# The opening of a two-layer diffusion step: a written-out order, squares summed by matmul, filter biases added by matmul

## Chip, core and metric

The kernel runs on one core of a Trainium2 chip. The metric is device time in microseconds (us), the median of three runs. A row of the trace is one execution taken by the hardware profiler. The core has TensorE (PE, whose weight loads are listed apart as PEld), VectorE (DVE), ScalarE (ACT), GpSimd (POOL) and SyncE (SP). SP and ACT here also issue transfers; an issue stands in their queue like any other instruction. Each engine takes its instructions in the order in which the program has them.

## What is computed

One inference step of a backbone with two layers, width 1024, on 512 latent tokens and 128 context tokens (640 columns in all). A layer is

```python
shift, scale, gate = split(silu(cond) @ W_mod + b_mod)      # one set for latents, one for context
h = rms_norm(x) * (1 + scale) + shift
u_a, g_a, u_b, g_b, u_c, g_c, m = split(h @ W_in)
y_a = GLU(S5_bidir(u_a)) * silu(g_a)                        # state-space scan in both directions
y_b = Hyena2(u_b) * silu(g_b)                               # long convolution with learnt filters, by FFT
y_c = MultiPool(u_c) * silu(g_c)
x = x + gate * W_out(sum_b sigmoid(m_b) * (y_b @ W_br_b))

# the filters of a layer (two orders x 512 channels) depend on weights alone:
f = sin(freq * (z @ w1 + b1)); f = sin(freq * (f @ w2 + b2))
filt = (f @ w3) * window                                    # then its Fourier transform
y = irfft(rfft(u) * rfft(filt)) + u * bias                  # bias folded into the filter's centre tap
```

The latent tokens get a position embedding before the first layer. All data are float32. Large products are made of three matmuls on a high and a low part of each operand.

## The kernel before

The 1024 features lie as 8 blocks (`kk`) of 128 partitions, tokens along the free axis in two halves of 320. A scheduler orders each engine's instructions from the program's order, from data dependences and from the number of buffers of each tile. Only the opening of layer 0 matters here, up to the first input product `u_a`, whose result the scan (S5) waits for. The pieces are these.

- `mlp` makes `fh`, the two sine layers under the filters (`fh_91` in the order rows).
- `load_x0` adds the position embedding to `X`. `square` squares each block and half on ACT (tile `sq`) and adds the squares up on DVE, so that one `acc` and one `sq` tile per half are left; `rsum` then makes their column sums by 20 matmuls (tile `ssq`), and `rinv` the reciprocal root and its copy over all partitions (`rdg`, `rbc`, `rr`).
- `mod_chunk` loads a fourth of the modulation weights of a shift or scale in four transfers of 512 KB (tile `wm`, four buffers), makes 8 matmuls (`modp`; a row of the trace counts two for each) and copies them (`mp`). `mod_turn` turns the result into columns (`modt`, then `smod` and `sg` on DVE). Chunks 0 and 1 are the shift, 2 and 3 the scale.
- `filter` makes one of four filters: five matmuls (`fw` x4, `fwp`), the window on DVE (`hx`, `hq`), two additions of a bias row (`br`, 1x256), `fold`, the split into `fhi`, `flo`, `fhp`, `flp` on ACT and DVE, 42 matmuls with the Fourier matrix (`fps`), copies (`hs`) and four stores (`hd`) in SP's queue.
- `s5_disc` and `s5_disc2` make the scan's coefficients (`pw`, `rs`, `bb`, `pi`, `po`, `ph`; stores `pwd`, `rsd`), much of it on ACT as copies. `s5_open` makes the scan's first matrices, with copies `bp` and `bf`.
- `make_h` makes `h` in 24 pieces, three column ranges for each block (`ht` on DVE, `hhi` on ACT, `hlo` on DVE; blocks 3 and 6 start on POOL), and `u_a` multiplies it with the first 512 columns of `W_in` in 192 matmuls (`mm`). Their weights arrive as `wr` and are split to `wh` (ACT) and `wl` (DVE). The result goes out as `ud` and comes back as `ug`, with which the scan's first matmul (`pz`) begins.

## Time and profile before

| | |
|---|---|
| median of 3 runs | 1528.59 us (1523.9 to 1529.53) |
| the profiled execution | 1527.04 us |
| its span, first to last instruction | 1525.3 us |
| mean granted TensorE clock | 0.982 |
| PE, DVE, ACT, POOL busy | 94%, 73%, 44%, 34% |
| first `u_a` matmul, last `u_a` matmul | 78.08 us, 128.14 us |
| first `pz` matmul | 145.3 us |

The span is 1.74 us shorter than the execution's own time. In the windows view a row is a stretch of the span: its length, then the busy time of each engine with the number of instructions, the granted TensorE clock (1.00 is full speed), the share of the DMA engines and GB/s.

### The profile page before, as it was taken

The page shows a single profiled execution, that of the slowest core. Times are in us where ns is not written, and L with a number is a line of the kernel's source. Part 1 is how long each engine was busy: PE and PEld are TensorE (multiplying, and loading weights), DVE is VectorE, ACT ScalarE, POOL GpSimd, SP SyncE. Part 2 cuts the span into 40 slices and gives each one's busy share as a digit, 9 for nine tenths or more (in the row PEclk, how much of TensorE's full clock was granted, in tenths as well). Part 3 has the DMA queues.
Part 4 walks back from the last instruction along what each step waited for, and adds up shares of the span by engine and source line. Part 5 has one row for each costly group of instructions (what it writes and reads, how often), then busy time and mean ns, then how long its engine had stood idle before and what let it go on. Part 6 is the DMA issues. An engine that isn't in the chain of part 4 may idle for free.

```text
span 1525.3 us, 28396 instructions
## 1 busy us (share of the span) xinstructions
PE 1441.0 (94%) x10812; PEld 1366.2 (90%) x10812; DVE 1107.4 (73%) x1962; ACT 672.7 (44%) x1454; POOL 514.9 (34%) x462
## 2 busy tenths in 40 slices
PE   3999999999999999999998998999999999999997
PEld 1688899999999998898897887999999999999996
DVE  7896987955777796544567779887567778866665
ACT  3474545434333344344334744544443334344443
POOL 0033435400343334553221444552004443266401
PEclk9799999999999999999999999999999999999998
DMA  9535222244222348543653442222522223322154
GB/s 317 185 109 145 78 69 75 70 129 122 92 79 70 94 127 273 173 149 125 205 177 109 136 119 77 79 74 91 162 85 80 84 70 111 111 84 83 39 176 153
DMA packets 121904, 182.41 MB, mean 120 GB/s; under 512 B 34104, under 2 KB 58440, under 8 KB 121257
## 3 DMA queue, kind: packets, MB, share of 16 engines
q1 hardware_dynamic: 117177, 174.25, 37.2%
q0 software_dynamic: 1152, 5.77, 1.2%
q8 instruction: 85, 1.39, 0.4%
q10 hardware_dynamic: 3440, 0.59, 0.2%
q14 instruction: 50, 0.41, 0.1%
HBM read 154.75 MB, written 25.80 MB: 118 GB/s over the span
## 4 chain that ended last, share of the span: by engine, by line
PE 67%; DVE 17%; DMA 5%; issue 5%; ACT 3%; POOL 2%; SPq 1%; POOLq 0%; DVEq 0%; ACTq 0%
PE mm L261 14%; PE mm L263 14%; PE mm L262 14%; PE mm L333 3%; PE mm L335 3%; PE mm L334 3%; DVE wl L239 3%; PE modp L404 2%; PE inva L1189 1%; PE invb L1189 1%; PE yp L1020 1%; DVE kk L1006 1%; DVE i L918 1%; DVE vx L1049 1%; DVE kk L1005 1%
## 5 line engine op out<-in xcount | busy, mean ns | idle before, releaser
L261 PE MATMUL mm<-hhi,wh 128*128 128x320 f32 x1408 | 442.0, 315 | 5.6 <-ACT raw L1040 2.7
L263 PE MATMUL mm<-hhi,wl 128*128 128x320 f32 x1408 | 438.7, 313 | 6.6 <-DVE wl L239 4.4
L262 PE MATMUL mm<-hlo,wh 128*128 128x320 f32 x1408 | 439.7, 312 | 1.0 <-DVE hlo L659 0.4
L239 DVE TENSOR_TENSOR wl<-wr,wh 128x512 fp32r<-128x512 f32 x316 | 262.8, 833 | 111.1 <-ACT wh L238 108.0
L238 ACT CAST wh<-wr 128x512 fp32r<-128x512 f32 x316 | 195.5, 619 | 260.7 <-PE mm L262 196.8
L261 PEld LDWEIGHTS mm<-hhi,wh 128*128 128x128 f32 x1408 | 266.9, 190 | 11.4 <-ACT raw L1040 4.3
L263 PEld LDWEIGHTS mm<-hhi,wl 128*128 128x128 f32 x1408 | 266.7, 190 | 8.9 <-DVE wl L239 5.9
L262 PEld LDWEIGHTS mm<-hlo,wh 128*128 128x128 f32 x1408 | 267.0, 190 | 3.2 <-DVE hlo L659 1.6
L261 PE MATMUL mm<-mhi,wh 128*128 128x320 f32 x256 | 79.7, 315 | 3.6 <-DVE X L1312 2.8
L262 PE MATMUL mm<-mlo,wh 128*128 128x320 f32 x256 | 80.1, 314 | 0.5 <-DVE mlo L242 0.4
L263 PE MATMUL mm<-mhi,wl 128*128 128x320 f32 x256 | 79.3, 313 | 0.4 <-DVE wl L239 0.4
L917 POOL TENSOR_TENSOR ow<-cw,po 128x512 f32<-128x512 f32 x32 | 38.9, 1233 | 109.0 <-PE yp L1020 101.3
L919 POOL TENSOR_TENSOR i<-i,i 128x1024 f32<-128x1024 f32 x16 | 43.9, 2747 | 69.3 <-DVE i L917 40.8
L239 DVE TENSOR_TENSOR wl<-ws,wh 128x512 fp32r<-128x512 f32 x48 | 42.2, 880 | 31.5 <-ACT wh L238 30.5
L1290 POOL TENSOR_TENSOR macc<-macc,mth 128x320 f32<-128x320 f32 x32 | 36.3, 1139 | 83.9 <-DVE mth L1288 83.8
L1288 DVE SCALAR_TENSOR_TENSOR mth<-mth,mm 128x320 f32<-128x320 f32 x64 | 31.1, 485 | 43.1 <-PE mm L263 43.1
L333 PE MATMUL mm<-hhi,wh 128*128 128x320 f32 x192 | 59.9, 312 | 0.0
L335 PE MATMUL mm<-hhi,wl 128*128 128x320 f32 x192 | 59.9, 312 | 0.0
L334 PE MATMUL mm<-hlo,wh 128*128 128x320 f32 x192 | 59.8, 311 | 0.0
L238 ACT CAST wh<-ws 128x512 fp32r<-128x512 f32 x48 | 29.8, 620 | 57.3 <-PE mm L262 29.6
L261 PEld LDWEIGHTS mm<-mhi,wh 128*128 128x128 f32 x256 | 48.5, 191 | 5.3 <-DVE X L1312 3.1
L1290 POOL TENSOR_TENSOR acc<-acc,mth 128x320 f32<-128x320 f32 x32 | 38.0, 1189 | 44.3 <-DVE mth L1288 34.3
(422 smaller groups left out, 3752.7 us busy)
## 6 DMA issues: line engine op xcount, KB each, us to landing
wr<-w_in SPq DMA_DIRECT2D x224, 256.0 KB, 2.9
wm<-w_mod SPq DMA_DIRECT2D x48, 512.0 KB, 4.7
wr<-w_out SPq DMA_DIRECT2D x48, 256.0 KB, 3.0
hd<-hs SPq DMA_DIRECT2D x32, 256.0 KB, 2.2
hsr<-hd SPq DMA_DIRECT2D x32, 256.0 KB, 2.8
mt<-kd SPq DMA_DIRECT2D x128, 32.0 KB, 1.8
wr<-w_br_a SPq DMA_DIRECT2D x16, 256.0 KB, 2.5
wr<-w_br_b SPq DMA_DIRECT2D x16, 256.0 KB, 3.2
```

The lines of the kernel that those rows point to most:

```text
L238: nc.scalar.copy(hi, src)
L239: nc.vector.tensor_tensor(out=lo, in0=src, in1=hi.bitcast(F32), op=ALU.subtract)
L261: nc.tensor.matmul(ps[i], wh[:, ks], at(hi, k, sl), start=(k == 0), stop=False)
L262: nc.tensor.matmul(ps[i], wh[:, ks], at(lo, k, sl), start=False, stop=False)
L263: nc.tensor.matmul(ps[i], wl[:, ks], at(hi, k, sl), start=False, stop=(k == kt - 1))
L333: nc.tensor.matmul(out, wh[:, ks], xh, start=(k == 0), stop=False)
L334: nc.tensor.matmul(out, wh[:, ks], xl, start=False, stop=False)
L335: nc.tensor.matmul(out, wl[:, ks], xh, start=False, stop=(k == 3))
L917: eng.tensor_tensor(out=out[:, r], in0=hb(r), in1=pb(0), op=ALU.mult)
L919: e.tensor_tensor(out=out, in0=out, in1=tmp, op=ALU.add)
L1288: v.scalar_tensor_tensor(out=o[:, sl], in0=th[:, sl], scalar=1.0, in1=ps, op0=ALU.add, op1=ALU.mult)
L1290: nc.gpsimd.tensor_tensor(out=acc[:, sl], in0=acc[:, sl], in1=th[:, sl], op=ALU.add)
```

## The change

Layer 0's opening is written in a new order, with explicit `issue_after` edges, which tell the scheduler not to place what stands inside before the instruction named. The sums of squares are made by 80 matmuls straight from the 16 `sq` tiles. The modulation chunks come in two pairs: (2, 0), then the first filter's 42 `fps` matmuls, then (3, 1). All four chunks are loaded through the same four `wm` buffers. `make_h` splits the columns at 512 (latent, context) in place of 320 and 512, which gives 8x2 pieces in place of 8x3. Two filters come before `u_a`, two between its four column tiles. The bias rows are loaded once for layer 0 and enter by two matmuls per filter, in both layers. The `hd` stores of layer 0 go out on ACT's queue. The transfer of `s5b` moves up to the second place on SP's queue, and the bias selector makes `cst` 128 columns wider.

```diff
@@ mod_chunk
-            nc.sync.dma_start(w, I['w_mod'][l, n, :, 2 * hf:2 * hf + 2, :])
+            self.last_wm = nc.sync.dma_start(w, I['w_mod'][l, n, :, 2 * hf:2 * hf + 2, :])
...
-        mp = M.tile([P, 512], F32, tag="mp", name="mp", bufs=1)
-        nc.scalar.copy(mp, ps)
+        mp = M.tile([P, 512], F32, tag="mp", name="mp", bufs=bufs // 2)
+        self.last_cp = nc.scalar.copy(mp, ps)
@@ filter
+            if t in (2, 4):
+                r = slice(0, 1) if t == 2 else slice(64, 65)
+                self.last_fw = nc.tensor.matmul(fp if t == 4 else fw[:, t], self.k(C_BR)[r], br[r], start=False,
+                                                stop=True)
...
-        v.tensor_tensor(out=hx[0:1, 2], in0=hx[0:1, 2], in1=br[0:1], op=ALU.add)
-        v.tensor_tensor(out=hq[64:65], in0=hq[64:65], in1=br[64:65], op=ALU.add)
...
-            nc.sync.dma_start(self.hd[l][o, r, :, hf], hs)
+            (nc.sync if l else nc.scalar).dma_start(self.hd[l][o, r, :, hf], hs)
@@ squares
+    def square_pe(self, X, kk, half, ps):
+        sq = self.N.tile([P, HT], F32, tag="sq", name="sq", bufs=2)
+        nc.scalar.activation(sq, X[:, kk, half * HT:half * HT + HT], AF.Square)
+        for j in range(nh):
+            c = half * nh + j
+            self.last_sq = nc.tensor.matmul(
+                             ps[:, c:c + 1], sq[:, j * 64:j * 64 + 64], self.k(C_ONE)[:, 0:1],
...
@@ s5_gen, the first two blocks
+        with ExitStack() as late:
+            if l == 0 and b < 2:
+                late.enter_context(self.tc.issue_after(self.cp0.ins))
+            nc.scalar.copy(bp[0:64, 0, :, :, 0:H], self.bb[0:64, :, gs, :])
...
@@ run
+                    mps = mods(2, 0, self.last_sq)
+                    dd = self.s5_disc(Q, SP)
+                    y = self.rinv((0, 1), nc.vector, "mm", ps=ssq, spread=False)
+                    with tc.issue_after(self.last_mp.ins):
+                        self.filter(0, 0, 0, F)
+                    turns(2, 0, mps, self.last_fw)
+                    with tc.issue_after(self.last_mt.ins):
+                        rr = self.rspread((0, 1), y, "mm")
+                    mps = mods(3, 1, self.last_f)
+                    turns(3, 1, mps, self.last_mp)
+                    with tc.issue_after(self.last_lo.ins), tc.issue_after(self.last_cp.ins):
+                        self.s5_disc2(Q, SP, *dd)
...
+                with tc.issue_after(self.last_mt.ins):
+                    self.filter(0, 0, 1, F)
+                self.make_h(0, X, ((0, LS, 0), (LS, T, 1)), rr)
+                uas = self.uas(SP)
+                with ExitStack() as late:
+                    for i in (self.last_wm, self.last_cp, self.last_f):
+                        late.enter_context(tc.issue_after(i.ins))
+                    self.cp0 = self.last_cp
+                    self.u_a(0, uas, range(1))
+                    self.filter(0, 1, 0, F)
+                    self.u_a(0, uas, range(1, 3))
+                    self.filter(0, 1, 1, F)
+                    self.s5_open(SP, 0, self.rsl)
+                    self.u_a(0, uas, range(3, 4))
```

The first place is PE from its first modulation matmuls on. Before, its rows are:

```order
L404 MATMUL modp<-wm,cs 32x512 x8
L415 MATMUL modt<-cst,mp 128x2 x4
L404 MATMUL modp<-wm,cs 32x512 x4
L511 MATMUL fw_667<-w_353,fh_91 128x256 x4
L511 MATMUL fwp<-w_353,fh_91 128x256
L404 MATMUL modp<-wm,cs 32x512 x4
L511 MATMUL fw_763<-w_353,fh_91 128x256 x4
L415 MATMUL modt<-cst,mp 128x2 x4
L404 MATMUL modp<-wm,cs 32x512 x6
L549 MATMUL fps<-fhp,frp 128x256
L404 MATMUL modp<-wm,cs 32x512 x2
```

In the changed program PE's rows from the second `mlp` product on are:

```order
L463 MATMUL mlpp<-mlp,w_117 128x320 x2
L609 MATMUL ssq<-cst,sq 64x1 x80
L406 MATMUL modp<-wm,cs 32x512 x16
L519 MATMUL fw_479<-w_152,fh_91 128x256 x3
L523 MATMUL fw_479<-br_154,cst 128x256
L519 MATMUL fw_479<-w_152,fh_91 128x256
L519 MATMUL fwp<-w_152,fh_91 128x256
L523 MATMUL fwp<-br_154,cst 128x256
L417 MATMUL modt<-cst,mp 128x2 x8
L664 MATMUL rbc<-rdg,cst 128x320
```

Chunks, filter products and Fourier products were mixed; now all 80 square sums come first, then two chunks together, then one filter's products. Between the rows above and the next ones stand only the first filter's 42 `fps` rows and the second `rbc`. The second place is PE at the end of that filter:

```order
L560 MATMUL fps<-flo,fr 128x256
L561 MATMUL fps<-fhi,fr 128x256
L406 MATMUL modp<-wm,cs 32x512 x16
L417 MATMUL modt<-cst,mp 128x2 x8
L519 MATMUL fw_689<-w_152,fh_91 128x256 x3
L523 MATMUL fw_689<-br_154,cst 128x256
L519 MATMUL fw_689<-w_152,fh_91 128x256
L519 MATMUL fwp<-w_152,fh_91 128x256
L523 MATMUL fwp<-br_154,cst 128x256
L559 MATMUL fps<-fhp,frp 128x256
L559 MATMUL fps<-fhi,fr 128x256
```

The second pair of chunks stands in one piece, and the second filter's products follow only after both chunks have been turned. The third place is ACT, where before the scan's copies stood among the first filter's pieces and a `mp` copy:

```order
L407 COPY mp<-modp 128x512
L802 DMA rsd<-rs 1024x1x32
L238 CAST fhp<-hq 128x256
L238 CAST fhi<-hc 128x512
L823 COPY pi<-pw 64x256
L824 COPY pi<-pw 64x256
L826 COPY po<-pw 64x256
L827 COPY po<-pw 64x256
L801 DMA pwd<-pw 2304x1x32
L823 COPY pi<-pw 64x256
L824 COPY pi<-pw 64x256
L826 COPY po<-pw 64x256
L827 COPY po<-pw 64x256
L238 CAST fhi<-hc 128x512
L407 COPY mp<-modp 128x512
```

In the changed program, from the last `mp` copies to the second filter's first cast, ACT's rows are:

```order
L409 COPY mp<-modp 128x512 x2
L836 DMA pwd<-pw 2304x1x32
L837 DMA rsd<-rs 1024x1x32
L858 COPY pi<-pw 64x256
L859 COPY pi<-pw 64x256
L861 COPY po<-pw 64x256
L862 COPY po<-pw 64x256
L858 COPY pi<-pw 64x256
L859 COPY pi<-pw 64x256
L861 COPY po<-pw 64x256
L862 COPY po<-pw 64x256
L850 COPY rsl<-rs 128x192
```

```order
L240 CAST wh<-wr 128x512 x3
L972 COPY bp_1234<-bb 64x8x16
L973 COPY bp_1234<-bb 64x8x16
L974 COPY bf_1236<-bb 128x8x16
L972 COPY bp_1238<-bb 64x8x16
L973 COPY bp_1238<-bb 64x8x16
L974 COPY bf_1240<-bb 128x8x16
L864 ACTIVATE pi<-pi 128x256
L885 ACTIVATE cw<-cw 128x512
L866 ACTIVATE po<-po 128x256
L693 ACTIVATE hhi<-ht,smod_168 128x512
L693 ACTIVATE hhi<-ht,smod_168 128x128
L693 ACTIVATE hhi<-ht,smod_168 128x512
L693 ACTIVATE hhi<-ht,smod_168 128x128
L240 CAST fhi<-hc 128x512
L240 CAST fhp<-hq 128x256
```

The copies and coefficient products of the scan moved behind the fourth `mp` copy and ahead of the second filter's `fhi` and `fhp`.

## Rows read from the trace of the kernel before

**Rows 1.** The page's head: span, and busy time of each engine.

```profile
span 1525.3 us, 28396 instructions
...
PE 1441.0 (94%) x10812; PEld 1366.2 (90%) x10812; DVE 1107.4 (73%) x1962; ACT 672.7 (44%) x1454; POOL 514.9 (34%) x462
```

**Rows 2.** Windows view: length, busy us and instructions by engine, clock, DMA share, GB/s.

```profile
20.00:30.00 10.00, 6.47 (x20) 1.88 (x20) 10.00 (x39) 4.54 (x12) 0.00 (x0) 1.00 1.04 401
...
36.50:56.00 19.50, 19.49 (x57) 9.08 (x59) 18.31 (x57) 7.54 (x14) 0.00 (x0) 0.50 0.68 224
56.00:80.00 24.00, 23.71 (x184) 19.05 (x180) 20.42 (x50) 15.57 (x34) 1.26 (x1) 1.00 0.46 159
...
100.00:130.00 30.00, 26.16 (x195) 25.20 (x197) 25.47 (x27) 17.95 (x45) 19.40 (x16) 0.94 0.40 115
```

**Rows 3.** Chain of waits, first 140 us: start, us, what.

```profile
31.72 4.75 DMA wm<-w_mod
...
62.09 2.44 PE ssq L599 x40
...
129.46 0.61 ACT ua L678
131.17 5.91 DMA ud<-ua
137.14 8.16 DMA ug<-ud
```

**Rows 4.** DVE by line and shape, 0 to 130 us: busy, mean ns, idle before.

```profile
L589 DVE TENSOR_TENSOR acc<-acc,sq 128x320 f32<-128x320 f32 x12 | 5.8, 486 | 0.0
L520 DVE TENSOR_TENSOR hx<-fw,wins 128x1024 f32<-128x1024 f32 x4 | 4.9, 1219 | 2.2 <-PE fw L511 2.2
...
L239 DVE TENSOR_TENSOR flo<-hc,fhi 128x512 fp32r<-128x512 f32 x12 | 8.2, 684 | 0.8 <-ACT fhi L238 0.7
```

**Rows 5.** ACT timeline around the filters' second sine: start, us, what.

```profile
36.97 0.74 ACT L464 ACTIVATE fh<-fh 128x640 f32<-128x640 f32 x1 [1.32 <-DVE fh L438]
37.73 0.52 ACTq L466 DMA_DIRECT2D fd<-fh  x1
38.30 0.47 ACT L582 ACTIVATE sq<-X 128x320 f32<-128x320 f32 x1 [0.60 <-DVE acc L589]
...
46.28 0.59 ACT L407 COPY mp<-modp 128x512 f32<-128x512 f32 x1 [4.59 <-PE modp L404]
```

**Rows 6.** PE timeline, modulation chunks and filter products.

```profile
25.96 4.20 PE L404 MATMUL modp<-wm,cs 128*32 128x512 f32 x16
...
46.12 3.78 PE L511 MATMUL fw<-w,fh 64*128 64x256 f32 x8
```

**Rows 7.** PE timeline, later places at the full clock.

```profile
61.02 0.28 PE L549 MATMUL fps<-fhi,fr 128*128 128x256 f32 x1
61.15 0.95 PE L415 MATMUL modt<-cst,mp 128*128 128x2 f32 x8
...
73.41 1.92 PE L404 MATMUL modp<-wm,cs 128*32 128x512 f32 x16
```

**Rows 8.** DMA issues on the page: KB each, us to landing.

```profile
wm<-w_mod SPq DMA_DIRECT2D x48, 512.0 KB, 4.7
```

**Rows 9.** ACT by line and shape, 0 to 100 us: busy, mean ns, idle before.

```profile
L823 ACT COPY pi<-pw 64x256 f32<-64x256 f32 x2 | 1.3, 652 | 1.3 <-DVE pw L697 1.3
...
L238 ACT CAST wh<-wr 128x512 fp32r<-128x512 f32 x3 | 1.7, 612 | 0.0
...
L934 ACT COPY bp<-bb 64x128 f32<-64x128 f32 x2 | 0.6, 297 | 0.0
...
L664 ACT ACTIVATE hhi<-ht,smod 128x320 fp32r<-128x320 f32 x6 | 3.1, 558 | 0.1
```

**Rows 10.** PE timeline at the end of the first input product.

```profile
128.00 0.31 PE L262 MATMUL mm<-hlo,wh 128*128 128x320 f32 x1
128.14 0.31 PE L263 MATMUL mm<-hhi,wl 128*128 128x320 f32 x1
```

More of the change, by code (lines that the diff above doesn't have):

```diff
@@ L116, in constants @@
     cst[:, CO[C_MAG]] = MAGIC
+    for r in (0, 64):
+        cst[r, CO[C_BR] + r] = 1.0 / (1.0 + f32(0.05))
     fmax = 15
@@ L531, in filter @@
                 hlo = F.tile([P, 2, 256], F32R, tag="flo", name="flo", bufs=2)
-                self.split(hhi, hlo, hc[:, r])
+                self.last_lo = self.split(hhi, hlo, hc[:, r])
             hs = F.tile([P, 2, 256], F32, tag="hs", name="hs", bufs=2)
@@ L550, in terms @@
             self.nc.tensor.matmul(out, w[:, 0], xl, start=False, stop=False)
-            self.nc.tensor.matmul(out, w[:, 1], xh, start=False, stop=(i == n - 1))
+            self.last_f = self.nc.tensor.matmul(out, w[:, 1], xh, start=False, stop=(i == n - 1))
     def fold(self, c, x, x23, e):
@@ L590, in square @@
             self.sacc[half] = [a]
+    def square_pe(self, X, kk, half, ps):
+        nc = self.nc
+        nh = HT // 64
+        sq = self.N.tile([P, HT], F32, tag="sq", name="sq", bufs=2)
[4 more added lines that the diff above has]
+                             ps[:, c:c + 1], sq[:, j * 64:j * 64 + 64], self.k(C_ONE)[:, 0:1],
+                             start=(half == 0 and kk == 0 and j == 0),
+                             stop=(half == 1 and kk == KD - 1 and j == nh - 1))
     def rsum(self, halves, tag):
@@ L668, in u_a, with uas @@
-    def u_a(self, l, S, uas):
+                nc.vector.scalar_tensor_tensor(out=tv, in0=X[:, kk, s:e], scalar=sg[:, kk, ci:ci + 1], in1=rv,
+                                               op0=ALU.mult, op1=ALU.mult)
+                nc.scalar.activation(hi, tv, AF.Identity, bias=b)
+                nc.vector.scalar_tensor_tensor(out=lo, in0=tv, scalar=b, in1=hi.bitcast(F32),
+                                               op0=ALU.add, op1=ALU.subtract)
+    def uas(self, SP):
+        uas = [SP.tile([P, NT, CW], F32, name=f"ua{i}") for i in range(2)]
+        for ua in uas:
+            self.nc.gpsimd.memset(ua[:, :, 64:65], 0.0)
+        return uas
@@ L669, in u_a @@
+    def u_a(self, l, uas, tiles):
         nc = self.nc
-        for i in range(4):
+        for i in tiles:
             ua = uas[i % 2]
-            nc.vector.memset(ua[:, :, 64:65], 0.0)
             def cb(half, ps, ua=ua):
@@ L815, in s5_vals @@
         nc.scalar.copy(t, rs[:, 0:6])
-        self.s5_open(S, l, t)
+        self.rsl = t
     def powers(self, pi, po, pw):
@@ new lines, in run, with mods @@
+                    self.mod_open(0, M)
+                    ssq = self.PS.tile([P, 512], F32, tag="mm", name="ssq", bufs=3)[0:64, 0:2 * (HT // 64)]
+                    for half in range(2):
+                        self.load_x0(X, half)
+                        for kk in range(KD):
+                            self.square_pe(X, kk, half, ssq)
+                    def mods(a, b, prev):
+                        with tc.issue_after(prev.ins):
+                            return [self.mod_chunk(0, n, M, "mm") for n in (a, b)]
@@ new lines, in turns @@
+                    def turns(a, b, mps, prev):
+                        with tc.issue_after(prev.ins):
+                            for n, mp in zip((a, b), mps):
+                                self.mod_turn(0, n, mp, "mm")
+                    mps = mods(2, 0, self.last_sq)
[3 more added lines that the diff above has]
+                        self.filter(0, 0, 0, F)
@@ L1383, in run @@
+                    turns(2, 0, mps, self.last_fw)
[5 more added lines that the diff above has]
+                        self.s5_disc2(Q, SP, *dd)
                 self.HP = eh.enter_context(self.pool("hp", side="left"))
                 self.new_h()
-                for half in range(2):
-                    self.make_h(0, X, half, rr[half])
@@ L1387, in run @@
-                for o in range(2):
-                    for hf in range(2):
-                        self.filter(0, o, hf, F)
+                with tc.issue_after(self.last_mt.ins):
[12 more added lines that the diff above has]
+                    self.u_a(0, uas, range(3, 4))
@@ L1435, in run @@
                                     self.filter(l + 1, 0, n // 2 - 2, F, fb() if n == 6 else None)
-                            rr = [r for r, _ in self.rinv((0, 1), nc.vector, "mm")]
-                            for half in range(2):
-                                self.make_h(l + 1, X, half, rr[half])
+                            rr = self.rinv((0, 1), nc.vector, "mm")
+                            self.make_h(l + 1, X, ((0, HT, 0),), rr)
+                            self.make_h(l + 1, X, ((HT, LS, 0), (LS, T, 1)), rr[:, HT:])
                             for hf in range(2):
@@ L1449, in layer @@
         with self.pool(f"s5{l}") as S:
-            uas = [SP.tile([P, NT, CW], F32, name=f"ua{i}") for i in range(2)]
-            self.u_a(l, S, uas)
+            if l:
+                self.u_a(l, self.uas(SP), range(4))
             self.load_u(l, S)
```

99 lines of the change are left out of this document (46 added, 53 removed).

## Prediction

> **What bounds the kernel now.** The page's head says that PE is busy 94% of the span [rows 1], but that is a mean over stages. The windows of the opening show another picture [rows 2]. From 20 to 30 us PE has 6.47 us of work, while DVE is busy for all 10.00 and the transfers run at 401 GB/s. From 36.5 to 56 PE is busy 19.49 of 19.50 us, but at a granted clock of 0.50. From 56 on the clock is 1.00 and PE and DVE are both nearly full. The chain of waits [rows 3] goes through both, and ends in a tail in which neither counts: copy `ua` at 129.46, store `ud` 5.91, load `ug` 8.16, after which the scan starts at 145.3. So the question is when `u_a`'s last matmul runs. Before it is at 128.14 [rows 10].
>
> In what follows T is the end of the square sums, L the first filter's last `fps`, M the last `modt`.
>
> **Squares, up to T.** Twelve additions of 486 ns leave DVE (5.8 us) [rows 4]. PE gets 80 matmuls for 20; 20 of them took 2.44 us [rows 3], so 80 cost 9.8. That lies under PE's idle time before 36 us, except for the last block's 0.6. If PE is still at the lower level there, five matmuls cost 1.2, and the last six blocks bunch up; that is the upper bound, T later by 3.5. T itself follows ACT, which has `fh` and then four squares at the end. DVE delivered `fh` at 36.97 with nine additions ahead of it; 36.97 - 9 x 0.49 = 32.6. What else leaves that part of DVE's row (phases, `wl`) and what comes in (coefficients) are both 4 to 6 us by the program's counts, so I take 33. X lands some 5 us later (2.1 MB more go ahead of it, at 401 GB/s), hidden by the coefficients that DVE now does first; without that cover T is up to 4 later. T = 33 + 0.74 + 0.52 + 4 x 0.47 + 0.6 [rows 5] = **37**, between 35 and 41.
>
> **First pair of chunks and first filter, T to L.** Chunk 2's weights wait in `wm`; it costs 1.92 at full clock, 4.20 at half [rows 6, 7]. Chunk 0's four transfers can start only as these matmuls free the four buffers. A transfer takes 4.7 us (median) and the chain shows 4.75 [rows 3, 8]. So the pair ends at T + 1.9 + 4.7 + 0.5 = T + 7.1, or T + 10 at half clock. The filter's products are five matmuls and two for the bias. The trace has no such one-row product; four `fw` of the same width took 3.78 us at half clock, so 0.95 each, and 0.47 at the full one. I take that as the nearest row and nothing as the lower end: 3.3 or 6.6. Then DVE needs `hx` (1.22), three `hc`, two folds, three `flo` of 0.68 each [rows 4], between casts on ACT; 42 `fps` at 0.12 us each (5.0) [rows 7] follow these pieces, in 8 to 10 us. L lies between T + 19 and T + 27; I take T + 22 = **59**. The old program was as far with this filter at 61.02 [rows 7], but had three chunks and three filters' products done by then, where the new one has two and one.
>
> **Second pair, L to M.** Chunk 3's weights are there; chunk 1's are asked for as chunk 3 runs. 1.92 + 4.7 + 0.5, a copy `mp` of 0.59 [rows 5] and two `modt` of 0.95 [rows 7] give M = L + 9.6. PE has nothing else in its row, so some 4 us of this are idle. Before, one such wait stood in the chain [rows 3], the other loads had filter products beside them. [...]
>
> **ACT ahead of the second filter.** Behind the fourth `mp` copy (ending at L + 7.7) ACT now has two store issues (0.52 each), eight copies `pi`, `po` of 0.65, `rsl` and three coefficient products (0.35 to 0.63, 1.8 in all), three casts `wh` of 0.61, six copies `bp`, `bf` of 0.30, and four `hhi`, two of 512 columns and two of 128, before `fhi` [rows 5, 9]. A 320-column `hhi` took 558 ns; the wide one lies between that and 893, I take 0.85, and 0.4 for the narrow one. Together 1.0 + 5.2 + 1.8 + 1.8 + 1.8 + 2.5 = 14.1. DVE's `hx` of this filter stands behind three `wl`, which wait for the casts. So the second filter's first `fps` runs near L + 22.5. PE has one filter's products (3.3) after M, and then waits from L + 13 to L + 22: **9 us idle**. Before, the same copies ran beside chunks and filter products. If ACT's copies were ready earlier they could not go earlier, because the engine keeps its row's order.
>
> **`make_h` and `u_a`.** `make_h` loses eight of 24 pieces, and DVE the bias additions, but ACT starts on `hhi` only at L + 20; the rest of its pieces with casts, `hs` copies and four store issues of about 0.5 are 18 us, so `hlo` ends near L + 40. By L + 42 PE has done 36 of the 192 matmuls and the third filter's products. Left are 156 x 0.147 [rows 10] = 23.0, two filters' 42 `fps` (10) and one filter's products (3.3): `u_a` ends at L + 78.5 = **137.5**, 9 us later than before.
>
> **From there to the end.** PE's row has 94 matmuls of the next products between `u_a` and the first `pz` before, 126 now. With the scan's first small groups (some 2.3) that is 126 x 0.147 + 2.3 = 20.8 us after `u_a`, where it was 17.2 with the load `ug` ending last [rows 3]. If PE sets the pace of the scan stage, the 32 more are 4.7 us of work done ahead, and the break-even is an end at 145.3 - 20.8 + 4.7 = 129.2. If the scan's own chain sets it, nothing is given back and the break-even is 124.5. That makes the loss 8.3 or 13; I take 9.5, nearer to the first because PE is busy in most of that stage. Layer 1 gets eight bias matmuls (0.47 each, 3.8) and loses eight short additions on DVE; between 0 and 3.8 I take 1.5. Sum: 1527.04 + 9.5 + 1.5 = **1538** us for an execution like the profiled one, which is 1.55 below the median. The store issues on ACT and the two single loads of bias rows are in the terms above or under them.
>
> **The rivals.**
> *Faster: DVE was the limit, and the opening gets dense.* DVE is full from 20 to 56 us and sheds the 5.8 us and the bias additions, and squares on PE may bring the clock up before the first chunk, where before 19.5 us passed at 0.50. For it speak those windows. Against it speak the two reloads and ACT's row. With no hole at all PE's work after T adds up to 74 us, so `u_a` would end at 111 and the time be 1510; with full clock and half of the holes it ends near 119 and the kernel takes 1518. It decides from an end before 124.5.
> *No change: the hole on ACT closes in part.* If the copies take 6 us less of PE's time, because `fps` of the second filter can begin earlier or `make_h` keeps pace with fewer pieces, `u_a` ends near 130 and the time is 1528 to 1533.
> *Slower still: the clock falls in the holes.* PE ran 16 `modp` records in 4.20 us after idle time, and in 1.92 when busy [rows 6, 7]. If the nine idle microseconds bring the lower level back, 18 us of matmuls run at half pace after them, which costs 9: 1547. The Trainium skill, page "TensorE: Matmul & The Clock Gate", section "HAM oscillation", says that waits for transfers between bursts bring the clock down again each time. By it this rival would be the rule; the window from 36.5 on, at 0.50 after a wait of 4.6 us for `wm`, agrees.
>
> **How the numbers follow.** A difference within 0.5% (7.6 us) can't be told from no change here. The forecast has a chance of 0.40, the rivals 0.25, 0.20 and 0.15, in their order. The forecast's own range is 1531 to 1545, of which a sixth lies within 0.5%. Faster: 0.25. Same: 0.20 + 0.07 = 0.27. Slower: 0.48. The range from 1512 to 1550 leaves out the dense opening in full, and several late cases together.
>
> **What would show it.** Right: in the changed trace `modp` waits for `wm` twice, near 40 and near 61 us; PE waits for ACT's `fhp` or `fhi` near 75 us for about 9 us; DVE's `acc` additions are gone; the last `mm` of `u_a` stands between 132 and 145, and the later stages are shifted by the same amount less 1 to 4 us. Wrong: if T is below 33 or L before 52, my step for DVE was too dear; if the reload wait is below 3 us, the price of a transfer; if the first `fps` of the second filter stands before L + 15, ACT's row. If `u_a` ends late and the total doesn't follow, the scan stage had room that I put too low.

## The result

The changed kernel takes 1569.58 us (median of 4 runs, 1566.31 to 1571.59), the kernel before 1529.06 beside it: ratio 1.0263, 95% interval 1.0225 to 1.0302. It is slower, as forecast, but the 40 us are nearly four times the forecast 11 (9.5 from the end of `u_a`, 1.5 from layer 1), and the time lies above the range's end of 1550.

### The profile after

The page's head, to be held against [rows 1]:

```profile
span 1567.7 us, 28626 instructions
...
PE 1475.4 (94%) x10964; PEld 1396.2 (89%) x10964; DVE 1096.7 (70%) x1912; ACT 674.9 (43%) x1445; POOL 513.5 (33%) x464
```

PE's share is still 94%: the share of the whole span says nothing of an opening that grew by 30 us. The windows of the opening do; columns as in [rows 2], with one stretch more, from 80 to 100 us.

```profile
20.00:30.00 10.00, 9.73 (x73) 8.47 (x73) 9.39 (x37) 3.90 (x9) 0.00 (x0) 1.00 0.96 358
36.50:56.00 19.50, 16.78 (x93) 8.41 (x92) 5.27 (x20) 2.60 (x6) 0.00 (x0) 0.91 0.65 217
56.00:80.00 24.00, 17.89 (x83) 11.02 (x84) 14.04 (x28) 5.72 (x11) 0.00 (x0) 0.65 0.54 182
80.00:100.00 20.00, 10.17 (x38) 5.75 (x34) 10.04 (x19) 14.74 (x31) 2.17 (x2) 0.59 0.29 73
100.00:130.00 30.00, 29.51 (x191) 27.82 (x192) 20.74 (x38) 17.52 (x37) 2.26 (x2) 0.93 0.29 91
```

One thing has to be known about the clock column. The trace has no entry of the granted clock before 42.9 us (in the kernel before: 28.7 us), and the view counts time without an entry as 1.00. By the durations of the matmuls (last section) PE ran at the lower level up to there, so the 1.00 and the 0.91 are too high.

Before, DVE was nearly full up to 56 us. Now it works 5.27 of 19.50 us between 36.5 and 56: it was relieved, and idles. From 56 to 100 us PE has 28.06 us of work in 44, at granted clocks of 0.65 and 0.59, so much of it at the lower level. Where PE stands still is in its timeline (start, us, what; in brackets the idle time before, and what ended it):

```profile
22.70 17.49 PE L609 MATMUL ssq<-cst,sq 128*64 128x1 f32 x160
40.12 3.27 PE L406 MATMUL modp<-wm,cs 128*32 128x512 f32 x16
46.11 4.90 PE L406 MATMUL modp<-wm,cs 128*32 128x512 f32 x16 [2.72 <-DMA wm<-w_mod]
...
52.44 0.69 PE L523 MATMUL fw<-br,cst 1*128 1x256 f32 x2
...
57.99 0.58 PE L559 MATMUL fps<-fhp,frp 128*128 128x256 f32 x1
...
67.98 1.92 PE L406 MATMUL modp<-wm,cs 128*32 128x512 f32 x16
76.02 5.16 PE L406 MATMUL modp<-wm,cs 128*32 128x512 f32 x16 [6.11 <-DMA wm<-w_mod]
81.11 1.95 PE L417 MATMUL modt<-cst,mp 128*128 128x2 f32 x16
...
88.17 1.21 PE L523 MATMUL fwp<-br,cst 1*128 1x256 f32 x2
97.27 0.58 PE L559 MATMUL fps<-fhp,frp 128*128 128x256 f32 x1 [7.89 <-ACT fhp L240]
...
100.49 0.58 PE L560 MATMUL fps<-flo,fr 128*128 128x256 f32 x1 [2.43 <-DVE flo L241]
```

The bracketed waits are 2.72 and 6.11 us for reloaded weights and 7.89 us for ACT's `fhp`; the gap in front of 100.49 is 2.43, for DVE's `flo`. In the terms of the prediction, T is 40.2 (end of `ssq`), L 67.9 and M 83.1, where 37, 59 and 68.6 were predicted. The second filter's first `fps` runs at L + 29. ACT's timeline shows what stood ahead of its `fhp`:

```profile
81.23 0.59 ACT L409 COPY mp<-modp 128x512 f32<-128x512 f32 x1 [10.64 <-PE modp L406]
...
81.84 1.18 ACTq L837 DMA_DIRECT2D rsd<-rs  x1
83.06 0.64 ACT L858 COPY pi<-pw 64x256 f32<-64x256 f32 x1 [1.24 <-issue]
...
87.51 0.62 ACT L862 COPY po<-pw 64x256 f32<-64x256 f32 x1
...
88.41 1.65 ACT L240 CAST wh<-wr 128x512 fp32r<-128x512 f32 x3
...
92.75 1.91 ACT L693 ACTIVATE hhi<-ht,smod 128x512 fp32r<-128x512 f32 x4
95.14 0.62 ACT L240 CAST fhi<-hc 128x512 fp32r<-128x512 f32 x1 [0.48 <-DVE hc L565]
96.81 0.40 ACT L240 CAST fhp<-hq 128x256 fp32r<-128x256 f32 x1 [1.05 <-DVE hq L533]
```

The row is the predicted one, two issues, eight copies, the casts and four `hhi`, then `fhi` and `fhp`. The first `u_a` matmul runs at 107.1 (before 78.1), the last store of `u_a` is issued at 154.7 (131.2). That is 23.5 us later. The scan stage of layer 0, taken to end where SP issues the load `yr` of its result, ends at 377.8 instead of 343.5: 34 us later. So 11 us more went between the first product and the scan's end. POOL's timeline shows a wait there that the kernel before did not have:

```profile
152.66 0.16 POOL L721 MEMSET ug<- 128x32 f32 x1 [43.23 <-DVE flo L241]
...
152.84 1.06 POOL L952 TENSOR_TENSOR ow<-cw,po 128x512 f32<-128x512 f32 x1
...
162.56 2.57 POOL L954 TENSOR_TENSOR i<-i,i 128x1024 f32<-128x1024 f32 x1 [3.13 <-ACT wh L240]
```

The fill of `ug` waited 43.23 us, by the record for a `flo` of the last filter. A fill with zeros reads nothing, so this is read as a wait for memory that a tile of that filter held before. The scan's matrices `ow` and `i` stand behind it. In the kernel before the fill waited for nothing:

```profile
100.52 0.17 POOL L687 MEMSET ug<- 128x32 f32 x1
...
114.20 2.49 POOL L919 TENSOR_TENSOR i<-i,i 128x1024 f32<-128x1024 f32 x1 [6.53 <-PE mm L262]
```

### The profile page after: what moved, and what is told of

Same layout as the page of the kernel before. It is cut to its first block, busy times and chain, and to the rows that moved or that the text cites. A ratio compares the mean times of both kernels' runs of the same rounds, so it can differ in the third digit from the quotient of the medians.

```text
span 1567.7 us, 28626 instructions
## 1 busy us (share of the span) xinstructions
PE 1475.4 (94%) x10964; PEld 1396.2 (89%) x10964; DVE 1096.7 (70%) x1912; ACT 674.9 (43%) x1445; POOL 513.5 (33%) x464
## 4 chain that ended last, share of the span: by engine, by line
PE 66%; DVE 16%; DMA 6%; issue 5%; ACT 3%; POOL 2%; SPq 1%; ACTq 0%; POOLq 0%; DVEq 0%
PE mm L263 14%; PE mm L265 14%; PE mm L264 14%; PE mm L335 3%; PE mm L336 3%; PE mm L337 3%; DVE wl L241 3%; PE modp L406 2%; DVE i L953 2%; PE inva L1227 1%; PE invb L1227 1%; PE yp L1058 1%; DMA wm<-w_mod 1%; DVE kk L1044 1%; DVE vx L1087 1%
## 5 line engine op out<-in xcount | busy, mean ns | idle before, releaser
L241 DVE TENSOR_TENSOR wl<-ws,wh 128x512 fp32r<-128x512 f32 x48 | 42.4, 884 | 32.2 <-ACT wh L240 31.3
L341 DVE TENSOR_TENSOR mth<-mm,mth 128x320 f32<-128x320 f32 x60 | 29.4, 490 | 32.3 <-PE mm L337 27.3
```

Of the source, the lines that this page charges most:

```text
L241: return nc.vector.tensor_tensor(out=lo, in0=src, in1=hi.bitcast(F32), op=ALU.subtract)
```

## The experiments

Each kernel was timed beside the kernel before (medians 1527.2 to 1531.0). The fill, the load of `ug` and the scan's end (issue of `yr`, layer 0) are times within the profiled execution, one for each kernel. Differences in us below are of medians; those of the ratios differ from them by up to 3 us.

| kernel | median us | ratio to before, 95% | `ug` fill | `ug` load | scan end |
|---|---|---|---|---|---|
| before | 1529.06 | 1 | 100.5 | 137.1 | 343.5 |
| changed | 1569.58 | 1.0263 (1.0225 to 1.0302) | 152.7 | 159.7 | 377.8 |
| e2_no_reload | 1548.17 | 1.0107 (1.0085 to 1.0128) | 136.3 | 144.4 | 361.3 |
| k1_reload_kept | 1553.64 | 1.0160 (1.0141 to 1.0180) | 139.8 | 145.5 | 362.8 |
| e3_copies_early | 1565.79 | 1.0225 (1.0203 to 1.0247) | 150.7 | 157.5 | 373.6 |
| e6_no_gates | 1550.47 | 1.0126 (1.0084 to 1.0167) | 136.0 | 144.6 | 361.5 |
| h1_between | 1549.32 | 1.0136 (1.0115 to 1.0157) | 138.4 | 145.8 | 362.4 |
| e1_filters_first | 1565.93 | 1.0241 (1.0207 to 1.0275) | 140.4 | 168.9 | 372.0 |
| f1_filters_first_no_gates | 1553.93 | 1.0159 (1.0138 to 1.0181) | 125.0 | 156.6 | 367.4 |
| e7_fill_late | 1570.95 | 1.0275 (1.0255 to 1.0294) | 155.2 | 162.2 | 378.9 |
| n1_fourth_earlier | 1561.04 | 1.0203 (1.0167 to 1.0239) | 141.6 | 167.2 | 367.7 |
| n2_fourth_last | 1573.42 | 1.0275 (1.0243 to 1.0308) | 162.0 | 165.3 | 383.2 |
| b1_bias | 1548.10 | 1.0129 (1.0100 to 1.0159) | 107.9 | 145.8 | 353.9 |
| b3_bias_l1 | 1531.87 | 1.0014 (0.9999 to 1.0029) | 102.0 | 135.3 | 342.0 |
| g1_bias_dve | 1560.81 | 1.0198 (1.0169 to 1.0226) | 147.2 | 154.6 | 371.5 |
| g2_bias_dve_no_gates | 1538.10 | 1.0052 (1.0031 to 1.0073) | 121.0 | 135.0 | 346.4 |
| g4_bias_dve_old_order | 1539.26 | 1.0054 (1.0031 to 1.0076) | 114.8 | 143.8 | 347.6 |
| k2_old_program | 1529.65 | 1.0009 (0.9992 to 1.0026) | 118.1 | 130.8 | 339.1 |
| b2_squares_pe | 1528.90 | 0.9997 (0.9984 to 1.0011) | 110.0 | 140.9 | 344.6 |
| k3_no_order | 1526.66 | 1.0001 (0.9990 to 1.0011) | 108.6 | 139.9 | 341.1 |

### The reload: e2_no_reload, k1_reload_kept

Each pair's second chunk takes its weights from the first's tiles, so chunks 0 and 1 are multiplied with the weights of 2 and 3. In e2 their eight transfers are left out; in k1 they still run, into a spare buffer that nobody reads.

```diff
@@ mod_chunk, e2
-            w = M.tile([P, 2, 512], F32, tag="wm", name="wm", bufs=bufs)
-            self.last_wm = nc.sync.dma_start(w, ...)
+            if bufs == 4 and n < 2:
+                w = self.wkeep[hf]
+            else:
+                w = M.tile(...); self.last_wm = nc.sync.dma_start(w, ...)
@@ mod_chunk, k1
+            spare = bufs == 4 and n < 2
+            w = M.tile([P, 2, 512], F32, tag="wx" if spare else "wm", name="wm", bufs=1 if spare else bufs)
             self.last_wm = nc.sync.dma_start(w, ...)
+            if spare:
+                w = self.wkeep[hf]
```

e2, expected: 

> The changed kernel, in which the second chunk of each pair multiplies with the first chunk's weights, so that 8 of the 16 modulation transfers of layer 0 and the wait for them are left out (the values of two chunks are wrong). Theory A (each reload stands in PE's row alone): the two waits for wm, 2.7 and 6.1 us, go, the turn of the second pair ends 8 to 12 us earlier, and so does everything after it: 1557 to 1562. Rival (behind the wait stands the first input's h, made by DVE and ACT, which sets the pace anyway): less than 3 us, 1566 to 1570.

k1, expected: 

> The changed kernel with the wait for the reloaded weights taken away but not their transfers: the second chunk of each pair multiplies with the first chunk's weights (wrong values), and its own four transfers of 512 KB still run, into one spare buffer that nothing reads. Without the transfers it took 1548.2. If the wait is the cost: 1546 to 1555 again. If the traffic is (it delays the input weights and the stores): 1562 to 1570.

Measured: e2 is 21 us below the changed kernel, which is more than either forecast, and k1 16, within its first forecast. The last `modt` runs at 67.6 and 69.6 us (changed: 83.1). So half of the loss hangs on the reload with all that follows from it, and by k1 most of that on the wait rather than on the traffic. In k1 PE's waits up to 130 us (engine, line, what ended the wait; total, times, longest) hold no `wm`, and the wait for ACT falls from 7.9 to 3.5 us:

```profile
PE fps L564 <- ACT fhp L240: 3.5, 1, 3.5
PE fps L565 <- DVE flo L241: 1.9, 3, 1.1
```

### The edges and ACT's copies: e6_no_gates, e3_copies_early, h1_between

e6 takes out every `issue_after` and leaves the program order. e3 puts `s5_disc2` ahead of the second pair, so that ACT's copies may run while PE waits. h1 keeps edges, but puts the products of a filter between the two chunks of each pair (the second filter's thus ahead of the fourth chunk's turn), the copies early, and the bias on DVE.

```diff
@@ e6: each of
-                    with tc.issue_after(...):
+                    with ExitStack():
@@ e3
+                    with tc.issue_after(self.last_lo.ins):
+                        self.s5_disc2(Q, SP, *dd)
                     mps = mods(3, 1, self.last_f)
                     turns(3, 1, mps, self.last_mp)
-                    with tc.issue_after(self.last_lo.ins), tc.issue_after(self.last_cp.ins):
-                        self.s5_disc2(Q, SP, *dd)
@@ h1
+                    mp2 = one(2, self.last_sq)      # one(n, after): mod_chunk behind an edge
...
+                    mp0 = one(0, self.last_fw)
...
+                    mp3 = one(3, self.last_f)
+                    with tc.issue_after(self.last_mp.ins):
+                        self.filter(0, 0, 1, F)
+                    mp1 = one(1, self.last_fw)
```

e6, expected: 

> The changed kernel with all its issue_after edges taken out: same instructions, squares on PE, bias by matmul, one load of the bias rows, two wide pieces in make_h, filters in the same program order, but each engine's row as the scheduler makes it. Theory A (the order is what costs): the opening gets back to that of before or better, 1522 to 1545. Rival (the pieces cost, above all 80 square matmuls and the matmuls for the bias): most of the loss stays, 1555 to 1570.

e3, expected: 

> The changed kernel, with the scan's coefficient copies allowed before the second pair of chunks (the edge behind the fourth mp copy is dropped, the one behind the first filter's flo kept). Theory A (ACT's row between the fourth mp copy and the second filter's casts is a hole of its own): PE's wait of 7.9 us for fhp falls below 3, and the time by 5 to 9, to 1560 to 1565. Rival (the copies only move to another place on the same path): the time stays within 3 us, 1566 to 1572.

h1, expected: 

> The changed kernel, written-out order kept, with four edits: the bias on DVE, each filter's products placed between the two chunks of a pair, the scan's copies allowed early, and the second filter's products no longer behind the fourth chunk's turn. By the single runs (bias 8.8, copies 3.8, the two reload waits 8.8 us and what stands behind them, up to 21): 1535 to 1545. A fixed order would beat the kernel before only if the squares' place at the head cost nothing either: below 1529.

Measured: all three missed their forecasts. Without edges the scheduler wins back 19 us; the time lies between the two forecasts. So does that of e3, which wins back only 4 (6 by the ratios), with an interval that overlaps the changed kernel's: PE's longest wait for `fhp` falls from 7.9 to 5.8 us, and what is left of it has other reasons than the copies. h1, which has the bias on DVE like g1 (below), gains 11 us on g1, which keeps the change's order, but stays 11 above g2, which has the bias on DVE and no edges, and 4 above its forecast. The order with better cover is better than the change's, and worse than none.

### Where the later loss sits: e1, f1, e7, n1, n2

The question was whether the scan stage waits for `u_a` or for the last filter. e1 puts both late filters ahead of `u_a`, f1 does the same without edges. e7 takes the fill of `ug` out of POOL's way (it goes behind the first `ow`). n1 and n2 move only the fourth filter.

```diff
@@ run, e1 (f1: and without edges)
-                    self.u_a(0, uas, range(1))
                     self.filter(0, 1, 0, F)
-                    self.u_a(0, uas, range(1, 3))
                     self.filter(0, 1, 1, F)
+                    self.u_a(0, uas, range(3))
@@ run, e7
-            self.load_u(l, S)
+            self.load_u(l, S, l > 0)                # layer 0: only the tile; fill and load later
...
                 g = self.s5_gen(l, b, S)
+                if l == 0 and b == 0:
+                    self.load_u(l, S)
@@ run, n1
                     self.filter(0, 1, 0, F)
+                    self.filter(0, 1, 1, F)
                     self.u_a(0, uas, range(1, 3))
-                    self.filter(0, 1, 1, F)
                     self.s5_open(SP, 0, self.rsl)
                     self.u_a(0, uas, range(3, 4))
@@ run, n2: the same line goes behind the last u_a
```

e1, expected: 

> The changed kernel, with the two filters of the second order placed ahead of the first input product again, not between its column tiles; all else as changed. Theory A (the scan's first matrices wait for the last filter, because POOL's zero fill of ug waits for the last filter's flo): that fill moves from 152.7 us to 120 to 135, the first pz from 177.9 to 165 to 170, and the time falls by 7 to 12 us, to 1558 to 1563. Theory B (the whole loss lies ahead of the first input product, in reload waits and the lower clock): the place of two filters changes nothing, 1566 to 1572.

f1, expected: 

> The changed kernel with both of its ideas of order undone at once: no issue_after edges, and all four filters ahead of the first input product. Without the edges alone it took 1550.5, with the place of the scan's fill of ug at 136.0 us. Theory A (edges and place of two filters are separate costs that add): the fill moves to 105 to 125, the scan stage gets 8 to 12 us shorter, and the time comes to 1536 to 1545. Rival (without edges the scheduler fills holes with these filters, so that moving them ahead only delays the first input product): within 4 us of 1550. What is left above 1529 is then the price of the pieces (squares, bias matmuls, stores on ACT).

e7, expected: 

> The changed kernel, in which only the two zero fills of ug and its load stand behind the scan's first block in the program, so that POOL makes the first output matrices ow before it waits for the last filter. Theory A1 (POOL's row is what is late: 5 us of ow products and the sums behind them): the time falls by 4 to 8 us, to 1562 to 1566. Theory A2 (the input matrices i are late too, since their buffers lie where the last filter's hs lay, and they decide): less than 2 us, 1567 to 1572.

n1, expected: 

> The changed kernel with the fourth filter moved up: behind the third, ahead of u_a's second tile (instead of behind its third tile). Theory F (the scan's first matrices wait for the last filter's buffers, and so the end of the last filter sets the pace of the scan stage): POOL's fill of ug, at 152.7 us in the changed kernel, comes at 130 to 142; the last store of u_a stays near 154 to 158; the end of layer 0's scan stage falls from 377.8 to between 363 and 370, and the time from 1569.6 to 1556 to 1563 us. Rival (the scan stage hangs on u_a's end alone): the fill moves as well, but the time stays within 1566 to 1573 us, later if u_a ends later.

n2, expected: 

> The changed kernel with the fourth filter moved back: behind the last tile of u_a (instead of behind its third). Theory F (the end of the last filter sets the scan stage): u_a's last store issues earlier, 143 to 148 us instead of 154.7, the fill of ug stays at 153 or comes later, up to 160, and the time is 1568 to 1577 us although u_a ends earlier. Rival (u_a's end sets it): the time falls with u_a's end, by 5 to 10 us, to 1559 to 1565 us.

Measured: in e1 the two effects nearly cancel, and the time falls between the two forecasts. The scan's data come 9.2 us later, the stage behind it gets 15 us shorter. f1 gains nothing on e6, as its rival had it: there the load of `ug`, 12 us later, outweighs the fill, 11 us earlier. e7 gives nothing: its first `ow` ran at 113.2, but the first sum `i` still at 164.9. So it was not the fill that held `i` up. n1 and n2 separate `u_a` from the last filter, and their times lie in the ranges of theory F. POOL's timeline of n1:

```profile
141.57 0.16 POOL L721 MEMSET ug<- 128x32 f32 x1 [31.74 <-DVE flo L241]
...
152.01 2.58 POOL L954 TENSOR_TENSOR i<-i,i 128x1024 f32<-128x1024 f32 x1 [3.67 <-ACT wh L240]
```

and of n2:

```profile
162.01 0.16 POOL L721 MEMSET ug<- 128x32 f32 x1 [49.14 <-DVE flo L241]
...
176.14 2.57 POOL L954 TENSOR_TENSOR i<-i,i 128x1024 f32<-128x1024 f32 x1 [7.36 <-issue]
```

n1's load of `ug` is 7.5 us *later* than in the changed kernel and its fill 11.1 earlier; its scan ends 10.1 earlier, and the ratio falls from 1.0263 to 1.0203. In n2 the last store of `u_a` goes out 5.3 us earlier (149.4), the last filter ends later, and the scan ends 5.4 later; the ratio (1.0275) is not to be told from the changed kernel's, but it did not fall with `u_a`. Both go with the last filter and against `u_a`. (n2's load of `ug` itself stood behind the late fill, at 165.3, so n2 alone does not tell the matrices from the load; n1 does.) In the changed kernel, e2, k1, e3, e6, e7, h1 and g1 the fill and the last store lie within 4 us of each other, and the scan ends 223 to 226 us after the fill. In n1 it ends 226.1 after the fill and 205.2 after the last store, in n2 221.2 and 233.8: the distance to the fill holds within 5 us, the one to the store does not. Where the fill comes 23 us and more ahead of the last store, as in before, b2, k3, g4, e1 and f1, the scan ends 206 to 217 us after that store.

What holds `i` up is not settled. In DVE's row of the changed kernel the first product of `i` runs at 159.9, behind three `wl` that follow the last filter's last `flo` (151.9). That it waits for memory of the filter's tiles and that the row merely has it there are both left by these runs.

### The bias matmuls: b1_bias, b3_bias_l1, g1_bias_dve

b1 is the kernel before with the bias entered by matmul in both layers, b3 the same in layer 1 alone. g1 is the changed kernel with the bias back on DVE.

```diff
@@ filter, b1 (b3: if l > 0 and t in (2, 4))
+            if t in (2, 4):
+                r = slice(0, 1) if t == 2 else slice(64, 65)
+                nc.tensor.matmul(fp if t == 4 else fw[:, t], self.k(C_BR)[r], br[r], start=False, stop=True)
...
-        v.tensor_tensor(out=hx[0:1, 2], in0=hx[0:1, 2], in1=br[0:1], op=ALU.add)
-        v.tensor_tensor(out=hq[64:65], in0=hq[64:65], in1=br[64:65], op=ALU.add)
@@ filter, g1: the same lines with + and - exchanged
```

b1, expected: 

> The kernel before, with the bias rows added by two matmuls per filter in both layers in place of two DVE additions (rows loaded as before, cst 128 columns wider). Forecast of the document: 16 one-row matmuls, some 3.8 us at full clock per layer, partly hidden: 1529 to 1534. Rival (DVE is the limit of the opening and loses 3.3 us there): 1525 to 1529. If the bias matmuls explain the 3.6 us that layer 1 lost in the changed kernel: 1532 to 1535.

b3, expected: 

> The kernel before with the bias by matmul in layer 1 alone. Theory D (direct cost: 8 matmuls of 0.62 us in a stretch where PE is full): the time rises by 4 to 7 us, to 1533 to 1537, and the opening stays as before. Theory E (no cost in layer 1, all 18 us of the run with both layers come from the opening): 1528 to 1531.

g1, expected: 

> The changed kernel with the bias rows added on DVE again in both layers (one load of the rows, order and edges as changed). On the kernel before, the bias matmuls alone cost 18 us. Theory A (they cost the same in the changed order): 1569.6 - 18, so 1549 to 1555. Rival (in layer 0 they cost so much only in the old, mixed order, where PE was full; in the changed order PE waits anyway, and only layer 1 counts): 1561 to 1566.

Measured: this piece alone costs 18 to 20 us in the old kernel (1.29%), far above all three forecasts, 10 of them by the end of layer 0's scan stage. Taken out of the changed kernel it gives back 9 to 10, as the rival had it. Layer 1 alone (b3) shows 2, with an interval (0.9999 to 1.0029) that still holds no change at all. A matmul of one row of 256 took 0.62 us at the higher level of the clock. Two things beyond that price were seen. First, the scheduler ordered the engines anew: in b1's ACT timeline

```profile
70.95 0.41 ACT L240 CAST fhp<-hq 128x256 fp32r<-128x256 f32 x1 [0.56 <-DVE hq L526]
75.03 0.62 ACT L240 CAST fhi<-hc 128x512 fp32r<-128x512 f32 x1 [3.67 <-PE fps L554]
76.06 1.07 ACT L546 COPY hs<-fps 128x512 f32<-128x512 f32 x2 [0.40 <-PE fps L554]
```

the cast `fhi` at 75.03 came 3.67 us after ACT ran dry, DVE's `flo` waited up to 7.0 us for such casts (before 0.7 in all), and the first `u_a` matmul ran at 86.6 instead of 78.1. Second, the clock. In the changed kernel the windows behind the fourth filter's bias matmuls (137 to 141 us; columns as above)

```profile
140.00:144.00 4.00, 4.00 (x18) 3.34 (x17) 3.89 (x8) 1.11 (x3) 0.00 (x0) 0.74 0.67 116
144.00:148.00 4.00, 4.00 (x25) 4.00 (x25) 2.37 (x4) 1.15 (x2) 0.00 (x0) 0.84 0.00 0
```

are granted 0.74 and 0.84 with PE busy for the whole time, while in g1, without those matmuls,

```profile
136.00:140.00 4.00, 4.00 (x28) 4.00 (x28) 3.94 (x9) 1.34 (x3) 0.00 (x0) 1.00 0.73 141
140.00:144.00 4.00, 4.00 (x31) 4.00 (x30) 2.71 (x5) 2.20 (x4) 0.00 (x0) 1.00 0.20 66
144.00:148.00 4.00, 4.00 (x34) 4.00 (x32) 1.39 (x2) 2.99 (x7) 0.80 (x3) 1.00 0.47 166
```

the clock stays at 1.00. That is one execution of each. The trace's own entry is 0.50 from 141.9 to 145.3 us, so by estimate 1.7 us of work were lost there. How b1's 18 us split between the two was not tried.

### The pieces without the order: g2, g4, k2, b2, k3

g2 is the changed kernel with the bias on DVE and no edges. g4 has also both late filters ahead of `u_a`. k2 goes on from there: loads, chunks (2, 3, 0, 1) and filters in the old program's order, while squares by matmul, the wide `make_h`, the single load of bias rows and `hd` on ACT's queue stay. b2 is the kernel before with the squares by matmul. k3 adds to b2 the single load and ACT's stores.

```diff
@@ run, k2
-                    mps = mods(2, 0, self.last_sq)
...
+                    self.filter_load(0, F, wins, fr, fh)
+                    self.mod_turn(0, 2, self.mod_chunk(0, 2, M, "mm"), "mm")
+                    self.mod_turn(0, 3, self.mod_chunk(0, 3, M, "mm"), "mm")
+                    self.s5_disc2(Q, SP, *dd)
+                    self.mod_turn(0, 0, self.mod_chunk(0, 0, M, "mm"), "mm")
+                    rr = self.rinv((0, 1), nc.vector, "mm", ps=ssq)
+                    self.mod_turn(0, 1, self.mod_chunk(0, 1, M, "mm"), "mm")
@@ run, b2 (k3: and br0, and hd on nc.scalar)
-                        self.square(X, kk, 0)
+                        self.square_pe(X, kk, 0, ssq)
```

g2, expected: 

> The changed kernel with the bias on DVE in both layers and without its issue_after edges. Theory A (the bias matmuls and the edges are the two costs, 18 and 19 us, and add): 1528 to 1536. Rival (they overlap, or the scheduler's rows differ again): 1540 to 1552.

g4, expected: 

> As the run without edges and with the bias on DVE, and all four filters ahead of the first input product: what is left of the change is squares on PE, one load of the rows, stores on ACT, wide pieces of make_h and the program order of the chunks. If none of these costs anything: 1526 to 1533, and below 1526 if the two savings of DVE and of make_h show at last. If the new program order of chunks and loads costs by itself: 1536 to 1552.

k2, expected: 

> All pieces of the change but the bias matmuls (squares on PE, one load of the bias rows, stores on ACT, early load of s5b, two wide pieces in make_h), in the program order of the kernel before and without edges. The same pieces in the changed program order took 1539.3 without edges. Theory O (the program order of loads and chunks costs the 9 us that are left): 1526 to 1533. Theory S (one of the pieces does, the stores on ACT's queue above all): 1536 to 1544.

b2, expected: 

> The kernel before, with the squares summed by 80 matmuls in place of DVE additions and 20 matmuls, in the old program order. In the changed kernel the 80 took 17.5 us, 1.07 for five, at the lower clock, and not 0.6. Theory P (PE has room before 36 us, DVE gets 5.8 us back): 1522 to 1529. Theory Q (they stand between other work on PE at half clock until 56 us and beyond, 10 to 17 us more in a stretch in which PE is full): 1534 to 1546.

k3, expected: 

> The kernel before with three pieces of the change and nothing else: squares summed on PE, one load of layer 0's bias rows (added on DVE), hd stores of layer 0 on ACT's queue. In the run of all pieces in the old program order the fill of ug came at 118 and the fourth ud at 126 us, and the first scan stage ended 4 us earlier than before, but layer 1, with the new make_h and rr tiles, gave it back. If that reading is right: 1522 to 1527. If the 4 us were the chance of one execution: 1527 to 1531.

Measured: g2 and g4 are 0.5% above the kernel before (g2 between its two forecasts, g4 in its second), k2, b2 and k3 not to be told from it (k2 as theory O, b2 at the end of theory P's range; k3's ratio of 1.0001 fits the reading that the 4 us were the chance of one execution). Nothing beat it. One path leads from the changed kernel to k2, in differences of ratios times 1529: bias back on DVE 9.9 us (g1), edges out 22.3 (g2), the old program order 6.6 (k2), rest 1.4. Each step is uncertain by 4 to 7 us, and along another path (e6 first: 21) the shares shift little.

## Why the prediction was right in sign and short in size

The profiled executions lie 42.4 us apart, where the sum had 11. Of the 31 us that it is short, some 14 lie before the end of `u_a` (terms that were too small), 10 between there and the end of layer 0's scan (a wait that it did not have), and 7 behind that.

**Squares, T.** In the range, at its upper end: 40.2. The lower level of the clock, which the bound allowed for, was there (five matmuls in 1.09 us, 17.49 in all). But the path was another: T was to follow `fh` on ACT, and not the last blocks but the whole row on PE sat on the end, with ACT's squares waiting for it. That the number fits is in part luck.

```profile
37.09 0.47 ACT L606 ACTIVATE sq<-X 128x320 f32<-128x320 f32 x1 [0.67 <-PE ssq L609]
```

**First pair and first filter, T to L.** T + 27.7, just beyond the upper end. The reload took 3.99 us in the chain of waits (I had 4.7), 2.72 of it a wait of PE, but both chunks ran for the most part at the lower level (3.27 and 4.90 us): the pair took 10.8 us where I had 7.1, and named 10 for that case. The `modt` and `rbc` products between filter and `fps` (3.3 us) were not in my term. The 42 `fps` took 9.9 us, 0.21 apart for most of it, near my 8 to 10.

**Second pair, L to M.** Predicted 9.6, measured 15.1. The chain names one transfer of 6.90 us where the row had 4.7, with three `wr` loads issued into that time, and the chunk behind it took 5.16 where I had 0.5 left. This step and the one before it (5.5 and 5.7 us short) are the most mis-sized ones before `u_a`.

**ACT ahead of the second filter.** Right: predicted 14.1 us from the `mp` copy to `fhi`, measured 13.3 (81.82 to 95.14), and 15.0 to `fhp`, for which PE waited; predicted 9 us idle, measured 7.9 and 2.4. Only the gain from mending it was not there to be had: e3 gives 4 us.

**`make_h` and `u_a`.** By L + 78.5 = 137.5 the product was to be done. ACT copies its last tile out at 153.9, L + 86: 9 of the 16 us come from L, 5.5 from the second pair, and 2 from the rest.

**From there to the end.** This step failed in its mechanism. It asked whether PE's pace or the scan's chain sets the stage, and priced the end of `u_a` alone: 9.5 us for 9. The runs showed a third party, the last filter, which the new order puts between `u_a`'s tiles. The fill of `ug` came 52 us later and the first sum `i` 48 us later than before; for a loss of 23 us at `u_a`, 34 came out at the scan's end. That the last filter sets this end, and not `u_a`, is shown by n1 and n2; whether the sums `i` wait for memory of its tiles was not tried by itself.

**Bias matmuls.** Priced at 0.47 each (0.95 at half clock) among a filter's products in layer 0, and at 1.5 us in all in layer 1. They took 0.62, and cost 9 to 10 us by g1, 18 by b1. I priced the instruction, not what it does to two other engines' rows.

**Behind the scan of layer 0.** The sum had 1.5 us for layer 1; the profiled executions lose 8 there (42.4 less 34.2). b3 accounts for 2 of them, the rest is open. From the scan's end to the end of the span it is 1181.7 to 1182.3 us in before, b2 and k3, 1185.4 to 1187.1 in g1, g2, g4, h1 and k2, and 1189.9 in the changed kernel. The second group also holds two small edits of layer 1 that the section on the change does not name: `rr` is one tile for both halves, and `ua` is filled with zeros on POOL instead of DVE. Some 4 us may hang on them; no run changes them alone, and these are single executions.

**The rivals.** Faster failed on its premises. DVE was relieved, and PE then waited for weights and ACT. Nor did the squares bring the clock up before the first chunk: PE worked on them nearly without a gap from 22.7 to 40 us (17.19 of 17.30 us busy), by their durations at the lower level to the end, and the clock's first entry, 1.00, begins at 42.9, within the first chunk. The squares alone (b2) give nothing: PE is then busy for all of 20 to 60 us and DVE for 33 of them, and the time stays. "Slower still" was partly the case: 0.65 and 0.59 granted between 56 and 100 us. The level was low after the waits (0.50 from 76 to 80 us, behind the 6.11 us for `wm`), as the Trainium skill has it ("TensorE: Matmul & The Clock Gate", "HAM oscillation"). But it was also low in stretches without any wait (0.50 from 60 to 64 us, and behind the fourth filter's bias matmuls).

## What to carry to other kernels

When an order is written by hand, list for every stretch what each engine has to do while the slowest piece is under way; two chunks through one set of buffers, back to back, leave a transfer uncovered that mixed work had hidden. Ask of every piece that is moved later who gets its memory: here the last filter held up the next stage, by its place and, as far as the record is read rightly, by the memory that the fill was to get, more than the product that the stage was to work on. And an engine that is full in the windows is a bound only if the work behind it was waiting for it: taking 6 us off DVE was worth nothing, and adding sixteen small matmuls to PE cost more than the DVE instructions that they replaced.

## What was not expected of the hardware

The view's granted clock says nothing where the trace has no entry. Its windows say 1.00 from 22.7 to 40 us in the changed kernel, but the 160 `ssq` records took 1.09 us for ten, against 0.61 in [rows 3]. The single `modp` records show where the level rose: in the changed kernel's first chunk those that start up to 41.8 us last 1.06 us each and those at 42.7 last 0.70 (0.59 to 0.62 in the chunk at 68.0); in the first chunk of the kernel before it is 1.06 up to 27.4 and 0.59 to 0.62 from 28.7 on. The clock's first entries begin at 42.9 and 28.7. So the 1.00 from 20 to 30 us in [rows 2] holds for the last 1.3 us alone. Where there is no entry, the durations are what can be read.

PE busy for all of a stretch didn't keep its clock: 0.50 from 60 to 64 us (busy 4.00 of 4.00), after `modt` products of two columns and the bias products. From 141.9 to 145.3 us it was down behind the bias products of the fourth filter, and stayed up in g1; behind those of the third filter, at 114 to 116 us, it did not fall. What makes the difference is open.
